# Half-row fetches, three-term products and twelve earlier slots in a hybrid decoder step

## The chip, the cores and the metric

The kernel runs on one core of a Trainium2 chip. The metric is device time in microseconds of one execution. Before the change the median of three runs is 1606.98 us (1599.02 to 1607.16). The core has a matrix engine (TensorE, PE in the profile, with its weight load shown apart as PEld), a vector engine (VectorE, DVE), a scalar engine (ScalarE, ACT), GpSimd (POOL), which also issues the indirect transfers, and SyncE (SP), which here issues most of the plain transfers. Sixteen DMA engines move the data.

## The reference

One layer of a decoder on 512 prompt tokens and 8 x 4 sample tokens. A projection feeds four retention heads and a convolution module; their outputs are mixed, added to the input and normalised, which gives `x1`. Then comes the part that the change touches, a retrieval of experts:

```python
q = (xb @ w_query).reshape(PEER_BLOCK, PEER_HEADS, PEER_DQ)
...
v1, i1 = lax.top_k(s1, PEER_TOPK)
v2, i2 = lax.top_k(s2, PEER_TOPK)
cand = (v1[..., :, None] + v2[..., None, :]).reshape(...)
sv, ci = lax.top_k(cand, PEER_TOPK)
idx = e1 * N_KEYS + e2
gate = jax.nn.softmax(sv)
u = jnp.take(peer_u, idx, axis=0)
act = jax.nn.gelu(jnp.einsum('phkd,pd->phk', u, xb), approximate=False)
vv = jnp.take(peer_v, idx, axis=0)
return jnp.einsum('phk,phkd->pd', gate * act, vv)
```

Each token picks 8 heads x 16 = 128 of 16384 experts. An expert is a row of 1024 numbers in each of two tables, `peer_u` and `peer_v`. The result is added to `x1` and normalised again.

## The kernel before, in words

The 544 tokens are treated in two ways. For 288 of them (128 first prompt tokens, the 32 sample tokens, 128 further prompt tokens) the chosen rows are **fetched**. For the last 256 (`ND`) prompt tokens all experts are computed **densely** and weighted with a matrix that is zero where an expert was not chosen.

*Fetched tokens.* `gather` (L567) handles a **slot** k: one chosen expert of each of 128 tokens. An indirect transfer on POOL's queue (L572) reads 128 rows of the joined table `uv` (8 KB each: 4 KB of `peer_u`, 4 KB of `peer_v`) into a tile `g`. DVE multiplies the first half with `x1` and sums it (the dot, L575), ACT makes the weight (L579, L580), and DVE adds the weighted second half to `acc` (L585). The tiles are three buffers in pool `gp`, and one more for some calls (`gx` for the first 60 slots, `gx2` in the last call), used for every fourth slot. There are 128 slots for the first prompt tokens (`I0`, in the profile `I`), 32 for the samples (`Is`: four experts of 32 tokens at a time) and 128 for the further prompt tokens (`Ib`).

*Dense tokens.* For each of 128 keys e, `scores_of` (L778) loads a 512 KB tile of the transposed first table and makes the 128 x 256 scores with 8 float32 products (L784). `v_stage` (L914) loads the matching 512 KB of `peer_v` into a tile `uv` (pool `uvp`, four buffers) and adds its 4 products of 128 x 512 to four accumulators `pB` (L920). The weight matrices are held in four buffers: `Gb` (keys 0 to 31), `Gc` (32 to 51), `Ga` (52 to 95), `Gd` (96 to 127). `build` (L855) makes the gate part of them out of one-hot factors: ACT makes `off` and `A` (L862, L864), DVE `M` and `B` (L866, L870), PE multiplies them (L875). `first_keys` (L888) does this for keys 0 to 95 and `last_keys` (L907) for 96 to 127. `s_stage` (L879) computes the scores of a key, applies Gelu and multiplies them into the buffer; it serves keys 32 to 51 inside `first_keys` and keys 96 to 127 late.

*Order.* The program's order is a suggestion: a planner simulates the program and writes down each engine's order of instructions, which is then fixed. Each engine takes its instructions strictly in that order. `phases` (L923) yields one `v_stage` at a time, with an `s_stage` of the last keys beside those after `last_keys` is through, and `run` (L965) alternates it with two slots of `fetched` (L944), which takes the 32 sample slots and then the 128 of the further prompt tokens. The **fence** (L576) is the last multiplication of `first_keys`: dots of the last call must stand behind it on DVE, and so must those of the sample call from slot `FREE` (12) on. At the end the two accumulator pairs are normalised and stored (L966).

Of the kernel before, what the change touches and what calls it, by code (L numbers as in the profile page):

```python
# [34 lines left out]
UV = 4  # L35
FREE = 12
EG = (32, 20, 44, 32)
# [56 lines left out]
def tile_step(ctx: ExitStack, tc: tile.TileContext, a, o):  # L94
# [472 lines left out]
    def gather(x1, idx, gate, acc, slots):  # L567

        for k in slots:
            spare = gx if x1 is x1_0 and k < KX else (gx2[0] if gx2 and len(slots) == 128 else None)  # L570
            t = (spare if spare is not None and k % 4 == 3 else gp).tile([128, 2 * D], F32, name="g")
            G.indirect_dma_start(out=t, out_offset=None, in_=a["uv"],  # L572
                                 in_offset=bass.IndirectOffsetOnAxis(ap=idx[:, k:k + 1], axis=0))
            act = gw.tile([128, 2], F32, name="act")
# [100 lines left out]
    for h0 in range(0, PH, 2):  # L675
        w = load_w(a["w_query"], h0 * 256)
        qq = small("qe", [128, 4, 128], bufs=1)
        for hs in ([h0], [h0 + 1]) if h0 == 0 else ([h0, h0 + 1],):
            for h in hs:
                for s in range(2):  # L680
                    m = (h - h0) * 2 + s
                    S.activation(qq[:, m], project(w, m, x1T0, 0, 128), AF.Copy)
            retrieve(lambda h, s: qq[:, (h - h0) * 2 + s], hs, 128, 1, E0, GT0, hs[0], led and (lambda ins: behind(ins, led[0])))
            ss = slice(hs[0] * TK, (hs[-1] + 1) * TK)
            c = V.tensor_copy(I0[:, ss], E0.rearrange("p h k -> p (h k)")[:, ss])
            led = led or [c]
# [103 lines left out]
    def topk_of(g, c0, which):  # L790
        w_, r_ = GSP[g]
        for h0 in which:
            retrieve(lambda h, s: qs[:, h * 2 + s, c0:c0 + w_], [h0] if r_ > 1 else [h0, h0 + 1], w_, r_, Eg[g], GTg[g], h0)
            ss = slice(h0 * TK, (h0 + (1 if r_ > 1 else 2)) * TK)
            V.tensor_copy(Ig[g][:, ss], Eg[g].rearrange("p h k -> p (h k)")[:, ss])

# [32 lines left out]
    for e in range(E0S[2], E0S[3]):  # L829
        S.activation(place(e), scores_of(e), AF.Gelu)  # L830
    gbs = ExitStack()
    gb = gbs.enter_context(tc.tile_pool(name="gb", bufs=1, side="right", reuse_waits="tile"))
    GW[0] = gb.tile([128, EG[0], ND], F32, name="Gb")
# [8 lines left out]
    dw_ = ctx.enter_context(tc.tile_pool(name="dw_", bufs=4, reuse_waits="tile"))  # L842
    gc = ctx.enter_context(tc.tile_pool(name="gc", bufs=1, reuse_waits="tile"))
    pacc = ctx.enter_context(tc.tile_pool(name="pacc", bufs=1, space=PSUM, reuse_waits="tile"))
# [62 lines left out]
    def last_keys():  # L907

        with tc.tile_pool(name="bt", bufs=2, reuse_waits="tile") as bt:
            for pt, ts in build(bt, E0S[3], EG[3], 16):  # L910
                S.activation(GW[3][:, :, ts], pt.rearrange("p t e -> p e t"), AF.Copy)
                yield

    def v_stage(e):  # L914
        vt = uvp.tile([128, D], F32, name="uv")
        nc.sync.dma_start(vt, a["uv"][e * NK:(e + 1) * NK, D:])
        W = place(e)
        for b in range(2):
            for q in range(2):
                T.matmul(pB[b][q], W[:, b * 128:(b + 1) * 128], vt[:, q * 512:(q + 1) * 512],  # L920
                         start=False, stop=(e == NK - 1), skip_group_check=True)

    def phases():  # L923
        for e in range(EG[0]):
            v_stage(e)
            yield
        gbs.close()
        gd = ctx.enter_context(tc.tile_pool(name="gd", bufs=1, side="right", reuse_waits="tile"))
        GW[3] = gd.tile([128, EG[3], ND], F32, name="Gd")
        b = last_keys()  # L930
        more = iter(range(E0S[3], NK))
        for e in range(E0S[1], E0S[3]):
            v_stage(e)
            if next(b, "end") == "end":
# [83 lines left out]
```

## Time and profile before

| | |
|---|---|
| median of three runs | 1606.98 us |
| the profiled execution | 1603.19 us, span 1601.4 us |
| mean granted TensorE clock | 0.971 |
| busy: PE, DVE, ACT, POOL | 93%, 77%, 38%, 23% of the span |
| moved by DMA | 503.75 MB, mean 315 GB/s |
| of that by indirect fetches (POOL's queue with some plain loads) | 305.12 MB |
| sample slots issued | 776.5 to 1065.3 us |
| last prompt slots (`Ib`) issued | 992.6 to 1567.4 us |
| v products (L920) | 949.6 us to 1585.9 us |
| score products (L784) | 492.1 us to 1406.9 us |

Times in the profile count from the start of the span. "Busy" for PE includes the drain of a product, so a busy PE need not be at its peak; where the pace of PE matters, the starts of successive instructions are compared. A float32 product appears as two instructions, each with a weight load. In a row that has "[0.60 <-ACT wgt L580]" the engine stood idle 0.60 us before the instruction, and what it waited for is named. A DMA share of 1.0 in a window means that all sixteen engines were busy with packets all the time.

### The profile page before, as it was taken

Reading aid. Unit: us, or ns where it says so; the run is one execution under the profiler, and the core shown is the slowest. Engines: PE = TensorE matmul, PEld = TensorE weight load, DVE = VectorE, ACT = ScalarE, POOL = GpSimd, SP = SyncE. Lnnn points to the kernel's source line nnn. Section 1 sums busy time; section 2 is a strip of 40 time slices with the busy share of each in tenths; the row PEclk is TensorE's granted clock in tenths of the full one; section 3 lists DMA queues with packets and bytes.
Section 4 is the critical chain, followed back from the end, with each engine's and each line's share of the span. In section 5 each row is a group of like instructions: output and inputs, shape, how many; then the busy total and the mean of one; then the engine's idle time right before and its main releaser. Section 6 shows DMA issues by size and latency. Waiting matters only on the chain.

```text
span 1601.4 us, 20802 instructions
## 1 busy us (share of the span) xinstructions
PE 1494.5 (93%) x7014; PEld 1010.1 (63%) x7014; DVE 1225.3 (77%) x3158; ACT 604.3 (38%) x1687; POOL 374.1 (23%) x335
## 2 busy tenths in 40 slices
PE   6899999996979999999999997999999999999996
PEld 6788556564756667788788875444566655543332
DVE  3939989989865999999852788566777777766666
ACT  2235542254222323333623888413994111111111
POOL 1001423444321222321120000122223222222221
PEclk9899999998989999999999997999999999999998
DMA  9458778997698669997794321998999999999995
GB/s 355 180 195 347 253 280 301 354 364 253 253 383 321 260 250 340 345 340 271 251 413 157 108 86 57 398 402 332 385 365 380 423 424 424 424 423 424 424 424 211
DMA packets 99543, 503.75 MB, mean 315 GB/s; under 512 B 10183, under 2 KB 21191, under 8 KB 56549
## 3 DMA queue, kind: packets, MB, share of 16 engines
q0 software_dynamic: 42240, 305.12, 48.7%
q1 hardware_dynamic: 50749, 189.96, 31.3%
q10 hardware_dynamic: 6448, 7.36, 1.5%
q8 instruction: 55, 0.90, 0.2%
q14 instruction: 51, 0.42, 0.1%
HBM read 497.03 MB, written 5.80 MB: 314 GB/s over the span
## 4 chain that ended last, share of the span: by engine, by line
PE 32%; DMA 28%; DVE 24%; issue 8%; ACT 4%; POOL 2%; SPq 0%; DVEq 0%; POOLq 0%; ACTq 0%
DMA g<-in_uv_dram,Ib 17%; PE pB L920 10%; PE sp L784 9%; PE mm L198 7%; DMA g<-in_uv_dram,I 7%; DVE acc L585 6%; DVE g L575 4%; POOL g L572 2%; ACT off L862 2%; PE mm L875 2%; PE mm L308 2%; DMA g<-in_w_in_dram 2%; DMA uv<-in_uv_dram 1%; DVE iu L504 1%; DVE score L505 1%
## 5 line engine op out<-in xcount | busy, mean ns | idle before, releaser
L784 PE MATMUL sp<-x1T,uv 128*128 128x256 f32 x2048 | 464.7, 384 | 15.4 <-ACT Ga L830 9.4
L784 PEld LDWEIGHTS sp<-x1T,uv 128*128 128x128 f32 x2048 | 385.5, 191 | 89.5 <-issue 23.2
L585 DVE SCALAR_TENSOR_TENSOR acc<-g,wgt,acc 128x1024 f32<-128x1024 f32 x285 | 365.0, 1281 | 99.3 <-ACT wgt L580 98.1
L572 POOL DMA_INDIRECT g<-in_uv_dram,I x128 | 181.9, 1421 | 435.1 <-DVE acc L585 222.6
L579 ACT ACTIVATE act<-act 128x1 f32<-128x1 f32 x288 | 57.9, 201 | 592.4 <-DVE g L575 592.0
L575 DVE SCALAR_TENSOR_TENSOR g<-g,x1g 128x1024 f32<-128x1024 f32 x160 | 195.3, 1224 | 94.2 <-DMA g<-in_uv_dram,Ib 63.1
L572 POOL DMA_INDIRECT g<-in_uv_dram,Ib x128 | 133.5, 1043 | 517.9 <-DVE acc L585 318.5
L575 DVE SCALAR_TENSOR_TENSOR g<-g,x 128x1024 f32<-128x1024 f32 x128 | 155.6, 1217 | 31.9 <-DMA g<-in_uv_dram,I 31.8
L198 PE MATMUL mm<-x1T,w 128*128 128x384 f32 (+1 forms) x512 | 176.1, 500 | 0.2 <-ACT score L524 0.2
L920 PE MATMUL pB<-uv,Ga 128*128 128x512 f32 x352 | 162.1, 604 | 1.1 <-DMA uv<-in_uv_dram 0.8
L862 ACT ACTIVATE off<-row,e1T 128x128 bf16<-128x128 bf16 x512 | 157.8, 388 | 1.5 <-PE mm L875 0.4
L198 PEld LDWEIGHTS mm<-x1T,w 128*128 128x128 f32 x512 | 96.6, 190 | 71.4 <-issue 37.9
L920 PE MATMUL pB<-uv,Gd 128*128 128x512 f32 x256 | 117.2, 601 | 2.1 <-DMA uv<-in_uv_dram 1.0
L920 PE MATMUL pB<-uv,Gb 128*128 128x512 f32 x256 | 115.4, 604 | 2.9 <-DMA uv<-in_uv_dram 2.5
L920 PEld LDWEIGHTS pB<-uv,Ga 128*128 128x128 f32 x352 | 63.7, 189 | 83.7 <-issue 63.1
L920 PEld LDWEIGHTS pB<-uv,Gd 128*128 128x128 f32 x256 | 46.1, 189 | 73.3 <-issue 48.2
L875 PEld LDWEIGHTS <-A 128*128 128x128 bf16 x1536 | 64.6, 100 | 36.6 <-issue 32.0
L920 PEld LDWEIGHTS pB<-uv,Gb 128*128 128x128 f32 x256 | 48.1, 193 | 59.6 <-issue 54.3
L875 PE MATMUL mm<-B,A 128*128 128x96 bf16 (+1 forms) x1536 | 68.4, 197 | 13.3 <-DVE Gc L901 12.4
L864 ACT ACTIVATE A<-off 128x1024 bf16<-128x1024 bf16 x64 | 67.4, 1053 | 28.1 <-PE mm L875 27.7
L870 DVE TENSOR_TENSOR B<-M,gtT 128x768 bf16<-128x768 bf16 (+1 forms) x192 | 69.8, 419 | 9.8 <-PE mm L875 9.6
L920 PE MATMUL pB<-uv,Gc 128*128 128x512 f32 x160 | 72.3, 599 | 0.0
(279 smaller groups left out, 1706.3 us busy)
## 6 DMA issues: line engine op xcount, KB each, us to landing
uv<-in_ut_dram SPq DMA_DIRECT2D x128, 512.0 KB
uv<-in_uv_dram SPq DMA_DIRECT2D x128, 512.0 KB
w<-in_w_in_dram SPq DMA_DIRECT2D x18, 1024.0 KB
w<-in_w_query_dram SPq DMA_DIRECT2D x16, 1024.0 KB
w<-in_w_out_dram SPq DMA_DIRECT2D x7, 1024.0 KB
g<-in_uv_dram,I POOLq DMA_INDIRECT x128, 7.9
keys<-in_state_retention_dram ACTq DMA_DIRECT2D x4, 512.0 KB
out_dram<-keys SPq DMA_DIRECT2D x4, 512.0 KB
```

The lines of the kernel that those rows point to most:

```text
L198: T.matmul(p[:, :n], w[m // 2][:, k, (m % 2) * 128:(m % 2 + 1) * 128], xT[:, k, c0:c0 + n], start=(k == 0), stop=(k == 7))
L308: mm = T.matmul(p[:n, q * 256:(q + 1) * 256], xT[:, k, c0:c0 + n], w[q][:, k, :], start=(k == 0), stop=(k == 7))
L572: G.indirect_dma_start(out=t, out_offset=None, in_=a["uv"], in_offset=bass.IndirectOffsetOnAxis(ap=idx[:, k:k + 1], axis=0))
L575: dot = V.scalar_tensor_tensor(t[:, :D], t[:, :D], 1.0, x1, op0=OP.mult, op1=OP.mult, accum_out=act[:, 0:1])
L579: S.activation(act[:, 1:2], act[:, 0:1], AF.Gelu)
L585: V.scalar_tensor_tensor(acc, v, wgt, acc, op0=OP.mult, op1=OP.add)
L784: T.matmul(sp, u[:, k], x1T[:, k, NG2:], start=(k == 0), stop=(k == 7))
L862: S.activation(off[:, t], row, AF.Abs, bias=e1T[:, t1 + t:t1 + t + 1])
L864: S.activation(A, off, AF.Relu, bias=1.0, scale=-1.0)
L870: V.tensor_tensor(B[:, q], M, pairs_of(gtT[:, q], t1).to_broadcast([128, TB // 2, ne, 2]), op=OP.mult)
L875: T.matmul(pt[:, t % nt], A[:, t - t1], B[:, q, (t - t1) // 2, :, t % 2], start=(q == 0), stop=(q == 2))
L920: T.matmul(pB[b][q], W[:, b * 128:(b + 1) * 128], vt[:, q * 512:(q + 1) * 512], start=False, stop=(e == NK - 1), skip_group_check=True)
```

## The change

1. A slot is fetched by two indirect transfers, one for each 4 KB half of the row: the table is viewed as twice as many rows of half the length, the indices are doubled when they are written (a `tensor_scalar` by 2.0 takes the place of a copy), and the second transfer has an element offset of one half row.
2. `v_stage` from key 52 on splits its operands. ACT copies the loaded tile to a float32r tile `vh` and the 128 x 256 weights to `Wh`; DVE subtracts to get the remainders `vl` and `Wl`, also float32r. Three products (`Wl` with `vh`, `Wh` with `vl`, `Wh` with `vh`) replace the one float32 product, so a key has 12 products of 128 x 512 in place of 4. Keys 0 to 51 are as before.
3. The split tiles live in a new pool `vhp` (two buffers of each), which takes the place of `Gc` once that has been used. To make this possible `Gd` is now the same buffer as `Gb`, and `gx2` moves to the other side of the memory.
4. `FREE` goes from 12 to 24: twelve more of the 32 sample slots may be worked on before the fence.

```diff
-FREE = 12
+FREE = 24
...
-            G.indirect_dma_start(out=t, out_offset=None, in_=a["uv"],
-                                 in_offset=bass.IndirectOffsetOnAxis(ap=idx[:, k:k + 1], axis=0))
+            for half in range(2):
+                G.indirect_dma_start(out=t[:, half * D:(half + 1) * D], out_offset=None, in_=a["uv"].rearrange("r (q d) -> (r q) d", q=2),
+                                     in_offset=bass.IndirectOffsetOnAxis(ap=idx[:, k:k + 1], axis=0), element_offset=half * D)
...
-            c = V.tensor_copy(I0[:, ss], E0.rearrange("p h k -> p (h k)")[:, ss])
+            c = V.tensor_scalar(I0[:, ss], E0.rearrange("p h k -> p (h k)")[:, ss], 2.0, None, op0=OP.mult)
...
-    gbs = ExitStack()
-    gb = gbs.enter_context(tc.tile_pool(name="gb", bufs=1, side="right", reuse_waits="tile"))
+    gb = ctx.enter_context(tc.tile_pool(name="gb", bufs=1, side="right", reuse_waits="tile"))
...
-    gc = ctx.enter_context(tc.tile_pool(name="gc", bufs=1, reuse_waits="tile"))
+    gcs = ExitStack()
+    gc = gcs.enter_context(tc.tile_pool(name="gc", bufs=1, reuse_waits="tile"))
...
         W = place(e)
+        if not vhp:
+            terms = ((W, vt),)
+        else:
+            vh, vl = vhp[0].tile([128, D], F32R, name="vh"), vhp[0].tile([128, D], F32R, name="vl")
+            S.activation(vh, vt, AF.Copy)
+            V.tensor_sub(vl, vt, vh.bitcast(F32))
+            Wh, Wl = vhp[0].tile([128, ND], F32R, name="Wh"), vhp[0].tile([128, ND], F32R, name="Wl")
+            S.activation(Wh, W, AF.Copy)
+            V.tensor_sub(Wl, W, Wh.bitcast(F32))
+
+            terms = ((Wl, vh), (Wh, vl), (Wh, vh))
         for b in range(2):
-            for q in range(2):
-                T.matmul(pB[b][q], W[:, b * 128:(b + 1) * 128], vt[:, q * 512:(q + 1) * 512],
-                         start=False, stop=(e == NK - 1), skip_group_check=True)
+            for w, v in terms:
+                for q in range(2):
+                    T.matmul(pB[b][q], w[:, b * 128:(b + 1) * 128], v[:, q * 512:(q + 1) * 512], start=False,
+                             stop=(e == NK - 1 and w is terms[-1][0] and v is terms[-1][1]), skip_group_check=True)
...
-        gbs.close()
-        gd = ctx.enter_context(tc.tile_pool(name="gd", bufs=1, side="right", reuse_waits="tile"))
-        GW[3] = gd.tile([128, EG[3], ND], F32, name="Gd")
+        GW[3] = GW[0]
...
+            if e == 52:
+                gcs.close()
+                vhp.append(ctx.enter_context(tc.tile_pool(name="vhp", bufs=2, reuse_waits="tile")))
...
-    gx2.append(ctx.enter_context(tc.tile_pool(name="gx2", bufs=1, reuse_waits="tile")))
+    gx2.append(ctx.enter_context(tc.tile_pool(name="gx2", bufs=1, side="right", reuse_waits="tile")))
```

More of the change, by code (lines that the diff above doesn't have):

```diff
@@ L794, in topk_of @@
             ss = slice(h0 * TK, (h0 + (1 if r_ > 1 else 2)) * TK)
-            V.tensor_copy(Ig[g][:, ss], Eg[g].rearrange("p h k -> p (h k)")[:, ss])
+            V.tensor_scalar(Ig[g][:, ss], Eg[g].rearrange("p h k -> p (h k)")[:, ss], 2.0, None, op0=OP.mult)
     for h0 in range(0, PH, 2):
@@ L912, in last_keys @@
                 yield
+    vhp = []
     def v_stage(e):
```

## The prediction

> **What bounds the kernel now.** I read the windows first (columns: length, busy time and count of PE, PEld, DVE, ACT, POOL, granted clock, DMA share, GB/s), to find which stages the change touches.
>
> ```profile
> 834.00:858.00 24.00, 24.00 (x113) 21.13 (x112) 0.38 (x1) 2.68 (x7) 0.94 (x1) 1.00 0.69 263
> 858.00:992.00 134.00, 118.30 (x1082) 101.57 (x1080) 101.59 (x381) 107.66 (x302) 0.00 (x0) 0.92 0.26 84
> 992.00:1092.00 100.00, 98.88 (x314) 44.41 (x315) 64.47 (x100) 33.66 (x98) 23.82 (x23) 0.98 0.95 373
> 1092.00:1199.00 107.00, 107.00 (x797) 60.00 (x797) 80.84 (x170) 89.94 (x262) 31.07 (x25) 1.00 0.94 365
> 1199.00:1407.00 208.00, 205.43 (x796) 127.50 (x794) 151.25 (x207) 50.88 (x175) 56.71 (x55) 1.00 1.01 415
> 1407.00:1582.00 175.00, 172.00 (x376) 67.36 (x375) 117.90 (x143) 23.78 (x95) 41.02 (x44) 1.00 0.99 413
> ```
>
> First keys run to the fence at about 992, sample slots to 1092, keys up to 51 to 1199; then a tail of 383 us holds keys 52 to 127 and the remaining slots, first with score products beside (to 1407), then without. Next the chain of waits (start, duration, what) for the tail, for the pace of PE, and the DMA view of 1400 to 1550:
>
> ```profile
> 895.98 1.04 PE mm L875 x24
> 897.01 3.52 PE sp L784 x16
> 1020.89 3.53 PE pB L920 x8
> 1024.78 3.53 PE pB L920 x8
> 1084.43 27.73 PE pB L920 x64
> 1522.89 11.42 DMA g<-in_uv_dram,Ib
> 1536.17 1.29 DVE acc L585
> 1537.72 11.42 DMA g<-in_uv_dram,Ib
> ```
> ```profile
> q0 software_dynamic: 5809, 42.31, 66.9%
> q1 hardware_dynamic: 5822, 21.22, 34.6%
> ```
>
> The tail's chain is transfer after transfer: 14.83 us from one to the next of the same buffer, four buffers, so 3.71 us for a slot, with all DMA engines busy. PE is close behind: 27.73/8 = 3.47 us for a key of v products, one key per slot. The two queues handle equal numbers of packets (5809 and 5822), 8 KB on POOL's queue and 4 KB on SP's. In engine time a slot (1.049 MB) costs 0.669 x 150 / 40.35 = 2.49 us, a tile (0.524 MB) 0.346 x 150 / 40.5 = 1.28 us; the shares sum to 1.015. How much the tail carries (dots with their accumulator reads, so two counts a slot; then the issues from 1199 to 1582):
>
> ```profile
> 1199.00:1407.00 208.00, 67.13 (x110) 1.00 1.01 415
> 1407.00:1582.00 175.00, 57.97 (x94) 1.00 0.99 413
> ```
> ```profile
> uv<-in_uv_dram SPq DMA_DIRECT2D x74, 512.0 KB
> uv<-in_ut_dram SPq DMA_DIRECT2D x27, 512.0 KB
> g<-in_uv_dram,Ib POOLq DMA_INDIRECT x99, 11.4
> ```
>
> So 102 slots are worked on and 99 issued, beside 101 tiles. (99 x 2.49 + 101 x 1.28)/1.015 = 370 of the 383 us: DMA bounds the tail, PE would bound it soon after, DVE has room. How DVE spends a slot there (idle before an instruction in brackets):
>
> ```profile
> 1538.06 1.22 DVE L575 SCALAR_TENSOR_TENSOR g<-g,x1g 128x1024 f32<-128x1024 f32 x1 [0.61 <-DMA g<-in_uv_dram,Ib]
> 1539.21 0.08 DVE L575 DVE_READ_ACCUMULATOR g<-g,x1g 128x1 f32 x1
> 1539.89 1.28 DVE L585 SCALAR_TENSOR_TENSOR acc<-g,wgt,acc 128x1024 f32<-128x1024 f32 x1 [0.60 <-ACT wgt L580]
> ```
>
> 1.15 us to the read, and 1.28: 2.43 us of work and 1.21 us of idle time, 0.60 for the weight and 0.61 for the next landing.
>
> **The change part by part.**
>
> *Twelve slots earlier.* They leave the tail and go ahead of the fence. Their gain in the tail is counted in its sum below: 87 issued, 90 worked on. Their new place:
>
> ```profile
> 833.09 1.28 DVE L585 SCALAR_TENSOR_TENSOR acc<-g,wgt,acc 128x1024 f32<-128x1024 f32 x1 [0.60 <-ACT wgt L580]
> 858.73 0.29 DVE L899 TENSOR_TENSOR Gb<-Gb,mm 128x128 f32<-128x128 f32 x1 [24.36 <-ACT Gb L835]
> POOL g L572 <- DVE Gc L899: 157.0, 1, 157.0
> ```
>
> The twelfth slot ends at 834 and DVE then idles 24.4 us until PE has made the scores of `Gb`; POOL's next issue waits 157 us for the fence. At 3.9 us a slot six of the twelve fit into that hole. The other six are 6 x 2.43 = 15 us of DVE in 858 to 992, where DVE is busy 102 of 134 us, and DMA is used to 0.26. The cover is PE's scores (118 of 134 us busy) and ACT (108). I charge +2 us; ends 0 (all covered) and +29 (none covered, 12 x 2.43). Behind the fence only 8 sample slots remain, so the last 128 begin some 50 us sooner; between 1092 and 1199 PE and ACT set the pace, and key 52 starts as before.
>
> *Two transfers a slot.* Bytes are the same. A 4 KB packet costs what a tile's does: 2 x 1.28 = 2.56 us of engines for a slot instead of 2.49. POOL issues twice:
>
> ```profile
> L572 POOL DMA_INDIRECT g<-in_uv_dram,I x128: 936/1071/7352, 129.7 to 738.1; - x128
> L572 POOL DMA_INDIRECT g<-in_uv_dram,Ib x128: 932/932/3545, 992.6 to 1567.4; - x128
> DVE g L575 <- DMA g<-in_uv_dram,I: 26.1, 22, 4.7
> ```
>
> One more issue is 0.93 us in the tail (POOL busy 41 of 175) and 1.07 us, at worst 7, in the front. There normalisations queue behind it on POOL, and later slots: perhaps six on the chain, 6 x 1.07 = +6 us at worst. Against it, a dot needs only the half issued first; DVE waited 26.1 us for landings between 130 and 500, and a quarter of that, 6 us, is the most I would credit. I take 0 for the front, ends -6 and +6. By packet counts, half-size packets give SP's tiles as many bytes as the slots where both queue, instead of half as many. In 1001 to 1036 PE started a key every 3.89 us (1020.89, 1024.78), waiting for tiles, instead of 3.53: nine such keys, -3 us. The doubled indices replace a copy by a multiply of the same size: nothing.
>
> The Trainium skill (DMA: Bandwidth & Descriptors, Queues, rings and completion order) says that each engine alternates between queues a packet at a time. The equal counts agree; what it would make of the tail is the second rival.
>
> *Three products.* No row shows a float32r product. A float32 one takes 3.47/4 = 0.87 us. The nearest row for a single pass is the bf16 one, 24 products of 96 columns in 1.04 us, or 0.231 us for 512 columns. I take 0.231 (the operands are rounded into float32r first, and the weight load of 0.19 us is shorter than that): 12 x 0.231 = 2.77 us for a key, instead of 3.47. The other end is 12 x 0.87 = 10.4 us.
>
> The Trainium skill (FP8 and Floating Point Precision, TensorE Precision Notes) says that true float32 makes four passes and that reduced float32 is truncated on reading; a quarter of 0.87 would give 2.60 us a key. No row here can show it.
>
> Each of the 76 keys adds work to ACT and DVE; nearest rows:
>
> ```profile
> L453 ACT ACTIVATE yt<-yt,lrs 128x1024 f32<-128x1024 f32 x2 | 2.5, 1240 | 9.6 <-DVE lrs L451 9.6
> L454 DVE TENSOR_TENSOR yt<-yt,lng 128x1024 f32<-128x1024 f32 x2 | 2.5, 1226 | 0.0
> L883 ACT ACTIVATE W<-sp 128x256 f32<-128x256 f32 x32 | 12.2, 380 | 52.0 <-PE sp L784 51.2 <-DVE Gd L886 0.8
> L886 DVE TENSOR_TENSOR Gd<-Gd,W 128x256 f32<-128x256 f32 x32 | 13.1, 422 | 1.8 <-ACT W L883 1.7
> ```
>
> ACT: 1.24 + 0.38 = 1.62 us a key, 123 us in a tail where it is busy 75 of 383; hidden, except that a slot's weight can queue behind a copy. DVE: successive instructions overlap by 0.08 us (1538.06 + 1.22 against 1539.21), so 1.14 + 0.34 = 1.48 us a key, 112 us. This stands on DVE's queue between dot and accumulation: a slot behind it comes later, and PE, which needed only the tile before, now waits for DVE.
>
> *The tail's new sum.* While scores are left (27 keys) PE needs 3.52 + 2.77 = 6.29 us a key, 170 us. DMA then moves 54 tiles (69 us) and, in what is left of 170 x 1.015, (172.6 - 69)/2.56 = 40 slots; DVE needs 40 x 2.43 + 27 x (1.48 + 0.34) = 146 us and fits. For the remaining 49 keys and 50 slots DVE needs 50 x 2.43 + 49 x 1.48 = 194 us, DMA (47 x 2.56 + 49 x 1.28)/1.015 = 180, PE 136: DVE bounds it. That is 364 us if subtractions fill the idle 1.21 us of every slot. ACT's queue costs some: 0.15 us a slot (a copy of 1.24 us in 4 us, half hit), 7 us. So 371 instead of 383: -12.
>
> *Memory.* The first split tile of key 52 waits for key 51's products on `Gc`, about 3 us once, hidden by score products already queued; `Gd` waited for `Gb` before too, as the pool was at the same place.
>
> **Sum.** -12 (tail) - 3 (tiles) + 2 (fence) + 0 (front) = -13 against the profiled 1603.2, whose span is 1601.4: 1590. The median of the runs stands 3.8 us above that execution, so 1594.
>
> **The rivals.**
>
> *First (slower): DVE's written order keeps its idle time.* If a subtraction stands ahead of a dot that has landed, or behind one that has not, idle time stays. Price: each idle 0.60 us kept in the 50 late slots adds 30 us to the 364, so 394, +11 with nothing else, near 1618; both kept, 425, near 1649. It decides from (383 - 364)/50 = 0.38 us per slot. For: DVE is strictly ordered and today idles 1.21 us in every slot. Against: the subtractions have two sets of tiles and can be placed in the holes.
>
> *Second (no difference): tiles first.* If both queues are always full, a tile comes every 2 x 1.28/1.015 = 2.52 us; 49 keys take PE's 2.77 us, 136 us, in which 29 slots are done, and 21 slots follow alone at 2.43 + 0.60: 64 us. With 170 and 7 that is 377, or 1600 to 1604. This is what the alternation named above leads to. Against: a key also needs DVE, whose order is written down.
>
> *Third (faster): DMA alone bounds the tail.* (87 x 2.56 + 101 x 1.28)/1.015 = 347, plus the 13 lost today: 360, -23; with -6 in front, 1575.
>
> *Fourth: the fence moves.* +15 to +29 instead of +2: 1607 to 1621. Against: the hole of 24 us.
>
> *Fifth: float32r is no faster.* From 0.33 us a product PE bounds the late part; at 0.87 it is over 500 us slower.
>
> **How the numbers follow.** My forecast 0.45 (own range 1583 to 1605), first 0.22, second 0.12, third 0.14, fourth 0.05, fifth 0.02. From no change a measurement tells about half a percent, 8 us, so faster means under 1599: 0.31 of my forecast, all of the third and a little of the second, 0.47. Same (1599 to 1615): 0.14, 0.10 and 0.04 of the first: 0.28. Slower: the rest, 0.25. The range: 1572, just under the third, to 1628, which holds the first with one hole kept and leaves out both kept.
>
> **What would show it.** A float32r product every 0.23 us; 24 sample dots ahead of 992 and the fence within some us of it; POOL's packets at 4 KB with as many bytes as SP's when both queue; in the tail DVE over 90% busy, PE with gaps that DVE ends, DMA below 1.0 after the scores. It is wrong if DVE keeps idle time per slot, if the last slots run alone, or if the fence is late by more than 10 us.

## The result and the profile after

The changed kernel takes 1649.72 us, median of four runs (1647.55 to 1656.95), against 1607.07 us of the kernel before measured beside it (four runs). The ratio is 1.0282, 95% interval [1.0242, 1.0322]: slower by 43 us where the prediction had 13 us faster, and above the range's end of 1628. The profiled execution took 1650.69 us (span 1648.9).

Landmarks come first. Rows of both kernels for one line each give count, minimum/median/maximum duration in ns, and the starts of the first and the last instruction: score products, the v products with `Gb` and `Gc`, and the copies into `Gd` of the kernel before,

```profile
L784 PE MATMUL sp<-x1T,uv x2048: 379/379/757, 492.1 to 1406.9; 128*128 128x256 f32 x187
L920 PE MATMUL pB<-uv,Gb x256: 592/592/1222, 949.6 to 1101.3; 128*128 128x512 f32 x128
L920 PE MATMUL pB<-uv,Gc x160: 592/592/676, 1101.7 to 1194.4; 128*128 128x512 f32 x160
L911 ACT ACTIVATE Gd<-mm x16: 573/577/597, 1101.9 to 1220.2; 128x512 f32<-128x512 f32 x16
```

and of the changed kernel (where `Gd` is the buffer `Gb`):

```profile
L785 PE MATMUL sp<-x1T,uv x2048: 376/379/634, 520.7 to 1462.3; 128*128 128x256 f32 x187
L937 PE MATMUL pB<-uv,Gb x256: 592/592/1219, 977.5 to 1126.1; 128*128 128x512 f32 x128
L937 PE MATMUL pB<-uv,Gc x160: 592/592/1200, 1126.5 to 1236.9; 128*128 128x512 f32 x160
L912 ACT ACTIVATE Gb<-mm x16: 570/576/597, 1141.6 to 1257.1; 128x512 f32<-128x512 f32 x16
L937 PE MATMUL pB<-vh,Wh x304: 387/389/632, 1254.6 to 1637.7; 128*128 128x512 f32 x152
```

The first score product comes 28.6 us later (520.7 against 492.1), before any key of the changed `v_stage` has run. `Gb`'s v products still are 28 us late at their start and 25 at their end; they take 148.6 us instead of 151.7. `Gc`'s last product is 42.5 us late, and the first copy into `Gd` 39.7. From the last `Gc` product to the last v product it is 400.8 us (1236.9 to 1637.7) instead of 391.5 (1194.4 to 1585.9). So the loss has three places: 28 us ahead of the scores (25 are left of them at the end of `Gb`), 17 more by the end of `Gc` (around 1126 to 1142), and 9 in the tail, where 12 were to be won. (That is 51.8 us at the last v product, of which the last normalisations give some back: 47.5 in the two spans.)

The same stages in the windows of the changed kernel (columns as in the prediction):

```profile
886.00:1018.00 132.00, 121.20 (x1107) 104.17 (x1105) 106.92 (x387) 109.58 (x309) 6.81 (x7) 0.95 0.38 131
1018.00:1118.00 100.00, 99.18 (x318) 44.83 (x318) 66.50 (x104) 35.47 (x103) 56.95 (x46) 0.99 0.94 359
1118.00:1242.00 124.00, 110.40 (x843) 61.81 (x842) 91.49 (x184) 96.54 (x285) 72.39 (x58) 0.94 0.98 368
1242.00:1462.00 220.00, 195.19 (x858) 150.78 (x857) 188.40 (x260) 81.58 (x218) 163.29 (x110) 0.97 1.00 392
1462.00:1592.00 130.00, 105.64 (x397) 76.01 (x397) 121.87 (x157) 59.66 (x128) 82.58 (x56) 0.95 0.97 373
1592.00:1638.00 46.00, 43.90 (x183) 33.05 (x181) 29.20 (x40) 20.27 (x29) 0.80 (x2) 1.00 0.46 147
```

In the tail DVE is at 94% (121.87 of 130) once the scores are through, as forecast. While scores run, DMA is full (1.00) and PE idles 25 of 220 us. Then comes what was not forecast: from 1592 no slot is left, the DMA share is 0.46, and the last keys run by themselves. It holds the subtractions of 15 keys, and the copies of ten of those keys (first and last of the ten) start 25.81 us apart, 2.87 us a key:

```profile
1606.50 1.06 ACT L927 ACTIVATE vh<-uv 128x1024 fp32r<-128x1024 f32 x1 [2.10 <-PE pB L937]
...
1632.31 1.06 ACT L927 ACTIVATE vh<-uv 128x1024 fp32r<-128x1024 f32 x1 [1.39 <-PE pB L937]
```

The new instructions, by form (count, then busy time and mean ns, then idle time before them):

```profile
L928 DVE TENSOR_TENSOR vl<-uv,vh 128x1024 fp32r<-128x1024 f32 x76 | 92.7, 1221 | 17.3 <-ACT vh L927 17.3
L927 ACT ACTIVATE vh<-uv 128x1024 fp32r<-128x1024 f32 x76 | 79.3, 1045 | 21.2 <-PE pB L937 20.1 <-issue 1.1
L937 PE MATMUL pB<-vl,Wh 128*128 128x512 f32 x304 | 104.1, 424 | 20.7 <-DVE vl L928 20.3
```

And the queues between 1300 and 1450 (packets, MB, share of sixteen engines):

```profile
q0 software_dynamic: 11033, 40.19, 67.1%
q1 hardware_dynamic: 5730, 20.88, 34.7%
```

Packets are 4 KB on both queues, but the slots' queue now sends 11033 of them and the tiles' 5730. Bytes stand at 2:1 as before. Engine time is 0.671 x 150 / 38.3 = 2.63 us for a slot (40.19 MB are 38.3 slots) and 0.347 x 150 / 39.8 = 1.31 us for a tile.

In front, GpSimd. For each kernel: the waits of its queue from 130 to 500 (total us, times, longest); then, from 130 to the first score product, the busy time of all engines, and DVE's dots alone (two counts a slot). Before:

```profile
POOL g L572 <- DVE acc L585: 179.1, 61, 8.4
```
```profile
130.00:492.10 362.10, 326.42 (x1391) 224.93 (x1390) 314.52 (x691) 136.85 (x348) 130.76 (x97) 0.95 0.86 317
130.00:492.10 362.10, 96.66 (x158) 0.95 0.86 317
```

And after:

```profile
POOL g L573 <- DVE acc L586: 53.3, 30, 4.7
POOL g L573 <- issue: 32.1, 105, 0.7
```
```profile
130.00:520.70 390.70, 331.45 (x1399) 228.14 (x1399) 331.37 (x720) 141.97 (x363) 241.28 (x190) 0.92 0.87 310
130.00:520.70 390.70, 104.03 (x170) 0.92 0.87 310
```

Before, GpSimd waited 179.1 us for accumulations, that is for a buffer to come free. After, it waits 53.3 us for them and is busy 241.28 instead of 130.76 us, with 0.3 us more between two issues (32.1 us in 105 gaps). The slots do not come slower by that: DVE has done the dots of 80 slots by 500 us in both kernels. It is the other work that comes late. Ahead of the first score product stand 85 slots' dots instead of 79; six slots at 2.43 us are 15 of the 17 us that DVE is busy longer, and it is idle 59 instead of 48 us.

### The profile page after: what moved, and what is told of

It is laid out like the page before. It is cut to its first block, busy times and chain, and to the rows that moved or that the text cites. A ratio compares the mean times of both kernels' runs of the same rounds, so it can differ in the third digit from the quotient of the medians.

```text
span 1648.9 us, 22151 instructions
## 1 busy us (share of the span) xinstructions
PE 1466.4 (89%) x7318; PEld 1079.2 (65%) x7318; DVE 1331.5 (81%) x3310; ACT 704.2 (43%) x1839; POOL 800.6 (49%) x623
## 4 chain that ended last, share of the span: by engine, by line
DVE 21%; PE 20%; DMA 11%; POOL 10%; issue 10%; ACT 7%; DVEq 0%; POOLq 0%; ACTq 0%
POOL g L573 10%; PE sp L785 10%; PE pB L937 5%; DMA g<-in_uv_dram,Ib 5%; DVE acc L586 5%; DVE g L576 4%; DMA g<-in_uv_dram,I 4%; ACT off L863 3%; PE mm L198 3%; DMA g<-in_uv_dram,Is 2%; PE mm L876 2%; DVE vl L928 1%; ACT A L865 1%; DVE iu L504 1%; DVE B L871 1%
## 5 line engine op out<-in xcount | busy, mean ns | idle before, releaser
L573 POOL DMA_INDIRECT g<-in_uv_dram,Ib x256 | 363.1, 1418 | 276.2 <-PE mm L876 110.9
L573 POOL DMA_INDIRECT g<-in_uv_dram,I x256 | 333.3, 1302 | 270.3 <-DVE acc L586 100.6
L576 DVE SCALAR_TENSOR_TENSOR g<-g,x1g 128x1024 f32<-128x1024 f32 x160 | 194.8, 1221 | 32.0 <-DMA g<-in_uv_dram,Is 17.0
L573 POOL DMA_INDIRECT g<-in_uv_dram,Is x64 | 77.1, 1205 | 98.5 <-DVE sv L506 35.9
L937 PE MATMUL pB<-vl,Wh 128*128 128x512 f32 x304 | 104.1, 424 | 20.7 <-DVE vl L928 20.3
L937 PE MATMUL pB<-vh,Wl 128*128 128x512 f32 x304 | 91.8, 417 | 30.6 <-ACT vh L927 27.9
L928 DVE TENSOR_TENSOR vl<-uv,vh 128x1024 fp32r<-128x1024 f32 x76 | 92.7, 1221 | 17.3 <-ACT vh L927 17.3
L937 PE MATMUL pB<-vh,Wh 128*128 128x512 f32 x304 | 98.6, 407 | 0.0
L937 PEld LDWEIGHTS pB<-vh,Wl 128*128 128x128 f32 x304 | 54.8, 193 | 58.3 <-ACT vh L927 43.5
L927 ACT ACTIVATE vh<-uv 128x1024 fp32r<-128x1024 f32 x76 | 79.3, 1045 | 21.2 <-PE pB L937 20.1
L937 PEld LDWEIGHTS pB<-vl,Wh 128*128 128x128 f32 x304 | 55.8, 195 | 49.6 <-DVE vl L928 39.9
```

Source lines behind the costliest of these rows:

```text
L573: G.indirect_dma_start(out=t[:, half * D:(half + 1) * D], out_offset=None, in_=a["uv"].rearrange("r (q d) -> (r q) d", q=2), in_offset=bas ...
L576: dot = V.scalar_tensor_tensor(t[:, :D], t[:, :D], 1.0, x1, op0=OP.mult, op1=OP.mult, accum_out=act[:, 0:1])
L927: S.activation(vh, vt, AF.Copy)
L928: V.tensor_sub(vl, vt, vh.bitcast(F32))
L937: T.matmul(pB[b][q], w[:, b * 128:(b + 1) * 128], v[:, q * 512:(q + 1) * 512], start=False, stop=(e == NK - 1 and w is terms[-1][0] and v ...
```

## The experiments

Diffs are against the kernel named in each. Each ratio is that of the kernel's runs to runs of the kernel before on the same chip, with its 95% interval.

**Which part costs: one part undone, one part alone.**

`whole_rows`: the changed kernel with one 8 KB transfer a slot.

```diff
-            for half in range(2):
-                G.indirect_dma_start(out=t[:, half * D:(half + 1) * D], ...)
+            G.indirect_dma_start(out=t, out_offset=None, in_=a["uv"], ...)
```

> The changed kernel with one 8 KB transfer a slot again; three products and 24 slots kept. Theory O (written order): the planner lets more slots go ahead of other work, and what stands behind them on a queue is late. Here 76 slots, as before the change (81 with halves), stand ahead of the last normalisation on POOL, so the first score product is back near 492 us (520 in the changed kernel); but 18 of the last call's weights still stand ahead of the first copy into Gd on ACT (4 before, 20 changed), so that copy stays 10 to 16 us behind PE's last Gb product, and 5 keys instead of 15 are left after the last slot: 1598 to 1612 us. Theory Q (the second issue on POOL is the whole loss, order matters little): all of it is given back, 1585 to 1597 us.

1607.62 us, ratio 1.0014 [0.9996, 1.0032]. The total lies in theory O's range, but the late copy that O needs is not there: the first copy into `Gb` starts at 1102.6, 3 us after `Gb`'s last product (1099.4). `halves_only` is the opposite, the kernel before with the two transfers (and doubled indices):

```diff
-            G.indirect_dma_start(out=t, out_offset=None, in_=a["uv"], ...)
+            for half in range(2):
+                G.indirect_dma_start(out=t[:, half * D:(half + 1) * D], ...)
```

> The kernel before with two transfers a slot and nothing else. Theory O: 81 slots ahead of the last normalisation, first score product near 520 us (492 before), 4 weights ahead of the first Gd copy, so nothing is lost there, and the last slots are bound by DMA as before: 1628 to 1642 us. Theory Q: the front loses the same 28 us, and every later slot is slower too, because POOL needs 2 x 1.9 us for it: 1645 to 1665 us.

1643.7 us, ratio 1.0251 [1.0216, 1.0286], between the two ranges. `no_split` is the changed kernel with the float32 product for all keys:

```diff
-            if e == 52:
-                gcs.close()
-                vhp.append(...)
```

> The changed kernel with the single float32 product for all keys; halves and 24 slots kept. Theory O: front late by 28 us, first Gd copy late by 15 us (20 weights ahead of it), then a tail with 12 fewer slots and PE at 3.47 us a key without DVE's subtractions: 1615 to 1630 us. If the three products were the loss instead: 1590 to 1605 us.

1646.04 us, ratio 1.0263 [1.0234, 1.0292], above both ranges. `free24_only` is the kernel before with 24 slots ahead of the fence:

```diff
-FREE = 12
+FREE = 24
```

> The kernel before with 24 slots ahead of the fence and nothing else. Theory O: the fence stays within 3 us of 992, but 18 weights stand ahead of the first Gd copy on ACT (4 before), which comes 10 to 16 us late, and the tail is 25 to 30 us shorter: 1588 to 1602 us. If the written order there costs nothing: 1574 to 1584 us.

1597.77 us, ratio 0.9954 [0.9938, 0.997], in theory O's range, though its first copy into `Gd` is not 10 to 16 but 3 us later than before (1104.6). So the two transfers carry the whole loss: without them nothing is left (1.0014), and alone they cost 2.5%. The twelve earlier slots by themselves gain 0.5%, the only part that does; the three products cost that much again (1.0014 against 0.9954; with two transfers a slot, 1.0282 against 1.0263, the intervals overlap).

To see where the transfers cost, `first_whole` is the changed kernel with whole rows in the first call (`I`) and halves in the two later ones:

```diff
-            for half in range(2):
-                G.indirect_dma_start(out=t[:, half * D:(half + 1) * D], ...)
+            if x1 is x1_0:
+                G.indirect_dma_start(out=t, out_offset=None, in_=a["uv"], ...)
+            else:
+                for half in range(2):
+                    G.indirect_dma_start(out=t[:, half * D:(half + 1) * D], ...)
```

> The changed kernel with one 8 KB transfer a slot in the first call and two of 4 KB in the other two. Theory A, the front carries nearly all of what two transfers cost: the first score product comes at 494-500 and the fence at 990-995 as with whole rows everywhere, and the rest is only the dearer packets (up to 10 us): ratio 1.002 to 1.008. Rival B, the later calls lose as much as the front (the copies into Gd, the longer issue beside the subtractions): first score product as in A, but ratio 1.012 to 1.020.

1613.69 us, ratio 1.0061 [1.0035, 1.0087]; the first score product comes at 495.4. Theory A holds: 1.0282 - 1.0061 = 0.022, 35 us give or take 8 by the intervals, is the first call's, and 1.0061 - 1.0014 = 0.005, 8 us give or take 5, that of the two later calls.

**Why the front is late.** The planner writes more slots ahead of each of the eight late normalisations in GpSimd's order (36, 51, 54, 61, 69, 71, 77, 81 instead of 34, 51, 54, 59, 66, 68, 72, 76). `pinned_front` is `halves_only` with the old counts enforced (50 for the second one).

```diff
+                if x1 is x1_0 and k >= AHEAD[0]:
+                    behind(fetch, norms[1 + sum(n <= k for n in AHEAD)])
```

> Two transfers a slot on the kernel before, as in halves_only, but the eight late normalisations of the front are pinned on POOL behind 34, 50, 54, 59, 66, 68, 72 and 76 slots, as in the kernel before (36, 51, 54, 61, 69, 71, 77 and 81 in halves_only). Theory O (the planner's order): the first score product is back at or before 500 us (492 before, 519 in halves_only), and the total at 1615 to 1628 us, the rest being the dearer 4 KB packets. Theory P (two issues occupy POOL for about 3 us a slot, so normalisations wait whatever their place): first score product at 508 to 519 us, total 1630 to 1645 us.

```profile
L785 PE MATMUL sp<-x1T,uv x2048: 379/379/757, 518.9 to 1435.5; 128*128 128x256 f32 x187
```
```profile
L789 PE MATMUL sp<-x1T,uv x2048: 379/379/483, 514.2 to 1425.3; 128*128 128x256 f32 x187
```

1628.8 us, ratio 1.0146 [1.012, 1.0172]. The first score product moves from 518.9 to 514.2, 5 of the 27 us there. That is within the scatter: in `no_split`, with the same counts as `halves_only`, it stands at 511.7. But the total falls by 1.0251 - 1.0146 = 0.0105, 17 us give or take 7; the profiled executions show 8 at `Gb`'s first product and 10 at the last v product. So the order bears on the loss, and how much the runs do not fix. The first score product is in theory P's range and the total between the two ranges. `tiny_second` is the kernel before with an added transfer of 256 bytes a row into an unused tile after each slot of the first call, and no halves:

```diff
+            if x1 is x1_0:
+                bit = gw.tile([128, 64], F32, name="bit", bufs=4)
+                G.indirect_dma_start(out=bit, out_offset=None, in_=a["uv"], ...)
```

> The kernel before with whole 8 KB rows, and in the first call a second indirect transfer a slot that brings 256 bytes a row into a scratch tile that nothing reads: POOL issues as often as with halves, and the packets of the rows stay whole. 72 slots stand ahead of the last normalisation (76 before). Theory P: first score product at 505 to 525 us, total 1620 to 1645 us. Theory O: with fewer slots ahead it comes at 480 to 496 us, and the total stays within 8 us of 1606 us.

Its score products and DVE's wait for slots (130 to 500):

```profile
L788 PE MATMUL sp<-x1T,uv x2048: 379/379/634, 533.8 to 1441.0; 128*128 128x256 f32 x187
```
```profile
DVE g L579 <- DMA g<-in_uv_dram,I: 43.2, 20, 6.9
```

1638.39 us, ratio 1.0224 [1.0195, 1.0252]. With a sixteenth of a half row and only 72 slots ahead of the last normalisation, the scores start later than in any other run, 533.8. So a second transfer is enough for such a loss, without bytes to speak of and with whole rows; whether GpSimd's time for the issue or its 128 further packets do it, this run does not separate. It does not repeat the front of the changed kernel either. The small transfers run ahead (the last is issued at 454.6), so all 128 of them stand ahead of the last normalisation, and here the slots are slower: 69 dots by 500 us instead of 80, with 43.2 us of waits for landings instead of 26.1. From 130 to 520 GpSimd is busy 276 of 390 us; up to 500 there are 36.8 us of gaps ahead of the small issues.

A second issue can hurt in two ways: normalisations queue behind it on GpSimd, or the slots themselves come slower. `halves_off_pool` and `whole_off_pool` take the normalisations off GpSimd, with two transfers and with one: the addition runs on DVE and the power of -0.5 is left out.

```diff
-        G.tensor_scalar(dst, var, EPS, None, op0=OP.add)
-        G.tensor_tensor(dst, dst, mhalf[:dst.shape[0]].to_broadcast(list(dst.shape)), op=OP.pow)
+        V.tensor_scalar(dst, var, EPS, None, op0=OP.add)
```

> The kernel before with two 4 KB transfers a slot, and the normalisations taken off GpSimd: the addition of epsilon runs on VectorE and the power of -0.5 is left out (so the normalised values are scaled otherwise and other experts are chosen; the work is the same). To be compared with the same edit on one 8 KB transfer. Theory P1, the front is late because normalisations queue behind the issues on GpSimd: the first score product comes within 8 us of the one with whole rows. Theory P2, the doubled issues slow the slots themselves, and with them the vector work ahead of the mix stage: 15 to 28 us stay between the two.

> The kernel before (one 8 KB transfer a slot) with the normalisations taken off GpSimd in the same way; the measure for the run with two transfers. By P1 the normalisations also waited behind single issues of about 1 us, so the first score product comes up to 8 us ahead of 492; by P2 within 3 us of 492, unless the planner writes another order.

```profile
L784 PE MATMUL sp<-x1T,uv x2048: 379/379/796, 522.9 to 1426.5; 128*128 128x256 f32 x187
```
```profile
L783 PE MATMUL sp<-x1T,uv x2048: 379/379/757, 502.5 to 1408.0; 128*128 128x256 f32 x187
```

20.4 us stay between the two, inside P2's band: most of the delay does not need the normalisations in GpSimd's queue. P2's reason does not hold either, as the slots are not slower: 81 dots by 500 us with two transfers, 80 with one. Ahead of the first score product stand 85 dots instead of 80, and five slots at 2.43 us are 12 us of DVE's time. So more slots are written and done ahead of the other work, with or without normalisations on GpSimd; what the rest of the 20 us is stays open. Neither of them started earlier than with the normalisations on GpSimd (the pair has other expert choices and an order of its own, so only the difference is used). 1632 and 1604 us, one execution each.

**The late copy into `Gd`.** In the changed kernel ScalarE's written order has 20 slot weights ahead of the first copy. `gd_ahead` puts the weights from the seventh slot on behind it.

```diff
+            if fence and len(slots) == 128 and k >= 6:
+                later.append(out)
...
+                for ins in later:
+                    behind(ins, gd)
```

> The changed kernel, with the weights of the last call's slots from the seventh on ordered behind the first copy into Gd on ScalarE (in the changed kernel 20 of them stand ahead of that copy, here 6). Theory Q, the written order of ScalarE costs the stage: in the changed kernel the copy runs at 1141.6, 15 us after PE has started its last Gb product (1126.1); here it follows that product within 5 us, Gc's last product starts near 1222 instead of 1237, and the total falls by about 15 us to 1630-1640. Rival R, the copy's place only shows that DMA and the slots are the limit there: Gc's products come sooner, but the slots held back are late by as much, and the total stays within 5 us of 1650.

The copies, and the window of PE's first idle time in the changed kernel, there and here:

```profile
L914 ACT ACTIVATE Gb<-mm x16: 570/575/597, 1125.8 to 1248.4; 128x512 f32<-128x512 f32 x16
```
```profile
1126.00:1145.00 19.00, 19.00 (x91) 9.01 (x90) 11.75 (x15) 5.58 (x18) 11.37 (x11) 1.00 0.86 307
```
```profile
1126.00:1145.00 19.00, 6.89 (x25) 3.09 (x24) 12.70 (x16) 3.95 (x14) 11.82 (x10) 0.70 1.01 402
```

The copy runs at 1125.8 and PE idles no more (busy 19.00 of 19 us, instead of 6.89). `Gc`'s last product starts at 1225.7 instead of 1236.9. But the total is 1646.65 us, ratio 1.0279 [1.0241, 1.0317], as in the changed kernel. Rival R holds: the late copy cost nothing that a measurement shows. DMA was full in that window (1.01); that the slots worked on meanwhile are missing later is the likely reason, and not shown.

**Why the three products gain nothing.** In `whole_rows`, without the halves, the tail from `Gc` to the last v product is 1201.0 to 1592.7, 392 us as before. Its two stretches, and the queues (packets, MB, share) in the first:

```profile
1201.00:1428.50 227.50, 197.02 (x874) 159.09 (x872) 188.21 (x257) 78.77 (x210) 83.29 (x56) 0.94 0.98 385
1428.50:1575.00 146.50, 126.02 (x512) 96.17 (x511) 142.43 (x188) 73.88 (x155) 51.89 (x31) 0.98 0.98 383
```
```profile
q0 software_dynamic: 7903, 57.54, 64.1%
q1 hardware_dynamic: 8198, 29.86, 33.8%
```

57.54 MB are 55 slots and 29.86 MB are 57 tiles: one slot for one tile, as before the change. 28 keys took 227 us, 8.1 us each. PE's waits from 1204 to 1595, and the largest wait of SyncE's queue in the first stretch:

```profile
PE pB L936 <- ACT vh L926: 32.0, 15, 3.8
PE pB L936 <- DVE vl L927: 18.1, 28, 1.4
```
```profile
SPq L781 <- DVE vl L927: 75.8, 14, 9.0
```

With 2.8 us for the weights' remainders PE waits 53 us, where the kernel before waited 1.8; the three products save 76 x 0.63 = 48. A tile's buffer now comes free when DVE has subtracted, no longer when PE is through with it, and the request for the next tile waits for that. The granted clock of 0.94 in the first stretch takes, by estimate, another 0.06 x 227.5 = 14 us of PE's full speed.

`five_tiles` gives `whole_rows` a fifth tile buffer.

```diff
-UV = 4
+UV = 5
-    dw_ = ctx.enter_context(tc.tile_pool(name="dw_", bufs=4, reuse_waits="tile"))
+    dw_ = ctx.enter_context(tc.tile_pool(name="dw_", bufs=3, reuse_waits="tile"))
```

> whole_rows with five tile buffers instead of four (and three instead of four buffers for the Gelu results of a key, to make room). Theory T (with scores left the tiles come too slowly, as four buffers share a queue that gets a third of the bytes): a key with scores takes 6.5 to 6.9 us instead of 7.5, the last score product comes at 1405 to 1418 us instead of 1428, total 1590 to 1602 us. Theory D (DVE bounds the tail throughout): last score product within 5 us of 1428, total 1603 to 1612 us.

```profile
1390.00:1536.00 146.00, 136.53 (x577) 107.77 (x576) 143.71 (x187) 76.74 (x155) 53.62 (x31) 0.99 0.98 380
1536.00:1600.00 64.00, 0.21 (x1) 0.00 (x0) 51.44 (x67) 9.94 (x40) 26.86 (x17) 0.54 0.79 290
```

```profile
q0 software_dynamic: 5807, 42.33, 58.2%
q1 hardware_dynamic: 7834, 28.50, 38.9%
```

1615.44 us, ratio 1.0066 [1.004, 1.0092], above both ranges. The queues are those from 1201 to 1389.5: 40 slots and 54 tiles, so the ratio follows the buffers (or the order that the planner writes for them). The last score comes at 1389.7 instead of 1428.4, so the supply of tiles did pace the keys. Now the keys end at 1536, DVE having been busy 143.71 of 146 us, and the slots left over run 60 us by themselves.

`split_late`, `split_112` and `split_odd` are `whole_rows` with the products in three terms only for keys 104 to 127, for keys 112 to 127, and for the odd keys.

```diff
-        if not vhp:
+        if e < 104:
```
```diff
-        if not vhp:
+        if e < 112:
```
```diff
-        if not vhp:
+        if e < 52 or e % 2 == 0:
```

> Whole rows and 24 slots, and the three products only for keys 104 to 127. In free24_only the slots end at 1532 us and PE goes on alone to 1588 us. If the split pays only where DVE and the tiles have room: 24 keys at 2.87 instead of 3.47 us are 14 us less, 1582 to 1592 us. If the split never pays: 1594 to 1606 us.

1599.74 us, ratio 0.9979 [0.9959, 0.9998]: no gain over 24 slots alone (0.9954), as the second range had it.

> The changed kernel with one 8 KB transfer a slot, 24 slots ahead of the fence, and the three products only for keys 112 to 127. With 24 slots alone the slots ended at 1532 and PE then ran 56 us by itself, 16 keys of 3.5 us. Theory T, the split pays once no slots run beside it: 16 keys of 2.87 us (the pace of the changed kernel's last keys) take 46 us, so the total falls 10 us below that of 24 slots alone, to a ratio near 0.989 (0.986 to 0.992). Rival U, a split key costs as much as a plain one wherever it stands, because its tile must land and be split before PE starts: 0.995 to 0.999, as when keys 104 to 127 were split (0.9979).

1597.74 us, ratio 0.9965 [0.9943, 0.9987]. In `free24_only` the slots are through at 1532 and PE then runs alone. A window after that, first of it and then of `split_112` (the number after POOL is the granted clock):

```profile
1534.00:1545.00 11.00, 11.00 (x27) 4.88 (x26) 4.96 (x8) 1.24 (x1) 0.80 (x2) 1.00 0.56 174
```
```profile
1534.00:1545.00 11.00, 8.74 (x25) 6.66 (x26) 7.47 (x12) 4.12 (x5) 0.80 (x2) 0.69 0.48 152
```

The split keys do run at 2.84 us each (four copies start at 1550.86 to 1559.39). But at the first of them PE waits 2.6 us for the copy and the subtraction (waits of PE from 1530 to 1590), and the granted clock of that window is 0.69:

```profile
PE pB L936 <- DVE vl L927: 1.6, 1, 1.6
PE pB L936 <- ACT vh L926: 1.0, 1, 1.0
```

The last v product stands at 1585.1 instead of 1588.2: of 16 x 0.63 = 10 us, 3 are left in the profiled executions. The wait and the slower clock, by estimate (1 - 0.69) x 11 = 3.4 us, account for most of the rest. The ratios don't tell the two kernels apart. Theory T had the pace right and not the total, which is rival U's.

> The changed kernel with one 8 KB transfer a slot and the three products only for the odd keys from 53 to 127; the even ones have the plain product. PE saves 38 x 0.63 = 24 us, and VectorE has half of the subtractions: 87 x 2.43 + 38 x 1.48 + 27 x 0.34 = 277 us in a tail of some 385, 72% instead of 88%. Theory D, VectorE's load made the split worthless (with all 76 keys it was 97 to 99% busy): with half of it the tail ends up to 20 us sooner than with 24 slots alone, ratio 0.982 to 0.990. Rival V, the order of tiles and slots sets the end (one slot for one tile, the last keys by themselves) and the split gives back in waits what it saves: 0.993 to 1.000, as with the last 24 keys (0.9979) and the last 16 (0.9965).

1607.61 us, ratio 1.0021 [0.9996, 1.0045], on the slower side even of rival V. ScalarE's copy of the tile, and what it waited for from 1204 to 1595, and the engines after the scores:

```profile
L926 ACT ACTIVATE vh<-uv 128x1024 fp32r<-128x1024 f32 x38 | 39.8, 1049 | 47.6 <-DMA uv<-in_uv_dram 47.6
```
```profile
1417.00:1546.00 129.00, 110.52 (x325) 63.79 (x324) 104.56 (x134) 38.11 (x100) 44.05 (x30) 0.95 0.99 396
```

In `whole_rows` DVE was the limit after the scores, as forecast (142.43 of 146.5 us). Here it is busy 104.56 of 129 us, 81%, and the kernel is no faster, so DVE's load alone is not the reason. The copies wait 47.6 us for tiles to land, and PE, which could start a plain product as the tile lands, waits for the copy: from 1200 to 1590 17.8 us for copies, 4.6 for subtractions and 11.1 for the plain keys' tiles, 33.5 us in all, where the split saves 24.

## Why the prediction was wrong

The forecast -13 was a sum of four terms. Two of them failed, and a third no run shows.

*The front, taken as 0 between -6 and +6: +28 at the first score product, +35 (give or take 8) in the total.* This step failed. It priced the second issue as "perhaps six on the chain, 6 x 1.07 = +6 us at worst". The slots took the second issues without delay: the 93 instructions more that GpSimd has up to the first score product take 110 us and the gaps 32, and its wait for free buffers gives way from 179 to 53 us. The row that said so was quoted (128 issues, 936/1071/7352 ns); what was left out was to add them, and to ask what stands beside the slots. That is the work that came late. Until the first score product DVE has six more slots to do, 15 us, and idles 12 us longer. The runs bound the causes: the old order of the normalisations gives back 5 us at the first score product and 17, give or take 7, in the total (`pinned_front`); 20 us stay with none of them on GpSimd. How much of the 28 us is the planner's order and how much GpSimd's time is not taken apart by a run. The credit for a first half that lands early did not show: DVE's wait for landings from 130 to 500 is 30.6 us instead of 26.1.

*The tail, taken as -12: 0 with whole rows, +9 as changed.* The duration of a product was right: 0.231 us forecast, 2.87/12 = 0.24 at the end, where keys run by themselves. A quarter of the float32 product, by the four passes that the Trainium skill (FP8 and Floating Point Precision, TensorE Precision Notes) states, was an estimate of 2.60 us a key and comes out 9% too short. The copies and subtractions were right too (1045 and 1221 ns for the large ones), and they filled DVE's holes after the scores (94%, and 97% with whole rows). So the first rival did not happen there; that its 1649, with both holes kept, meets the measured 1649.72 is luck, as most of the loss lies in the front.

What failed is the step "DMA then moves 54 tiles and, in what is left, 40 slots" in 170 us. With whole rows it was 57 tiles and 55 slots in 227 us, from `Gc`'s end to the last score. The other division by itself costs the sum nothing: at the forecast's prices (57 x 1.28 + 55 x 2.49)/1.015 = 207, and 34 slots and 48 keys are left, 34 x 2.43 + 48 x 1.48 = 154 for DVE, 361 in all instead of 364. The term that was mis-sized is the price of a transfer. 1.28 and 2.49 were read where nothing was split; beside the split the engines, 0.98 busy, moved 385 GB/s instead of 415, by which the 207 us become 223 of the 227. `five_tiles` had the forecast's own load, 54 tiles and 40 slots, and took 188 us. Why transfers take longer beside the split no run takes apart. And PE did not set the pace, but waited 53 us for copies and subtractions, about what the three products save. When the slots are through early, the last keys run alone (15 in the changed kernel, with DMA at 0.46); moved the other way (`five_tiles`), the slots run alone. "The last slots run alone" was named as a sign against the forecast; in the changed kernel it was the last keys.

*The tiles, -3:* `Gb`'s 32 keys take 148.6 instead of 151.7 us, but 150.7 in `halves_only` and 152.3 in `no_split`, which have the same packets. So no run shows this term. The second rival stood on equal packets of two queues that are always full (the alternation that the Trainium skill states in DMA: Bandwidth & Descriptors, Queues, rings and completion order); the counts are 11033 to 5730. The packet times of the traces show that "always full" failed. Before the change, from 1250 to 1400, at least two packets of each queue are in flight all the time, and 5815 and 5813 start. After it, from 1300 to 1450, that is so in 0.66 of the time, in which 5857 and 5358 start; for the rest one queue, nearly always the tiles', has next to nothing in flight. This agrees with an alternation while both have work, but does not prove it: in `whole_rows` 4983 and 6582 start in such times (1201 to 1428.5), and the records don't tell one engine's packets from another's.

*The fence, +2:* the 24 slots stand ahead of it, and `free24_only` reaches `Gb`'s products at 949.1 instead of 949.6 us and issues the first slot of the last call at 990.4 instead of 992.6. Nothing at the fence, then, and inside the ends; but `Gc`'s last product comes 7.5 us later (1201.9 instead of 1194.4), which no term held. The sign "the fence is late by more than 10 us" did come (1018), by way of the front.

*Packets of half the size:* as forecast, 2.57 us a slot in `halves_only` from 1300 to 1450 (0.672 x 150 / 39.2) for 2.56, and 1.28 a tile. The rest of the 2.63 of the changed kernel goes with the split: beside it whole rows take 2.64 (and tiles 1.34) in the same stretch. The two later calls cost 8 us. The longer wait for `Gd`, forecast as nothing, was 16 us at the copy and nothing in the total (`gd_ahead`).

The faster kernel of this study is `free24_only`, 0.9954. It frees the slots 49 us sooner (last accumulation 1532.3 instead of 1581.6), but PE then bounds the tail, so little of that reaches the end.

## What to carry to other kernels

Price an added issue by its sum over the stage and not by those that happen to be quoted on the chain. Hold that sum against the issuing engine's waits, which may take it up for the fetched data themselves, and look at what other work stands behind the issues in the engines' order: here that work was late and the slots were not. Take the price of a transfer from a stretch in which the new work runs beside it. Here, with the DMA engines full, slots and tiles came about one to one with four buffers of each, and 40 to 54 with five tile buffers. The faster products gained nothing, as PE waited for copies and subtractions for as long as it saved, and these held each tile's buffer until DVE was through.

## What the runs showed of the hardware that was not expected

GpSimd's indirect issues have no fixed length. From 1300 to 1450 (count, busy us and mean ns, idle time), first `free24_only` and `whole_rows`, both with one 8 KB transfer a slot, then `pinned_front`, with two of 4 KB and no subtractions:

```profile
L572 POOL DMA_INDIRECT g<-in_uv_dram,Ib x41 | 41.9, 1021 | 111.3 <-DVE acc L585 95.8 <-DMA g<-in_uv_dram,Ib 15.5
```
```profile
L572 POOL DMA_INDIRECT g<-in_uv_dram,Ib x38 | 57.9, 1522 | 94.0 <-DVE acc L585 92.6 <-DMA g<-in_uv_dram,Ib 1.3
```
```profile
L575 POOL DMA_INDIRECT g<-in_uv_dram,Ib x79 | 108.0, 1368 | 40.6 <-DVE acc L590 21.7 <-issue 18.3 <-DMA g<-in_uv_dram,Ib 0.6
```

1021 ns without the subtractions and 1522 with them; but 1368 in `pinned_front`, where DVE is busy 105 of 150 us, as in the kernel before (106), whose issues take 933. So neither the subtractions nor a higher load on VectorE is needed for a long issue. The Trainium skill (SBUF — State Buffer, Who interferes with whom) says that a two-input `tensor_tensor` shares only a read interface with GpSimd and, as an inference, doesn't stall the writing of descriptors; these runs neither bear that out nor contradict it. What sets the length was not tried.

Transfers moved less in the same time beside the split, with the engines as busy: from 1300 to 1450 424 GB/s in the kernel before (DMA share 1.02) and 394 in `whole_rows` (0.99).

In `split_112` the granted clock fell after two waits of PE of 1.0 and 1.6 us, in a stretch at 1.00. Windows of 2 us read 0.62, 0.50 and 0.50 from 1536 to 1542, the last two with PE busy all the time, and the window from 1545 to 1548 reads 1.00 again; that is the 0.69 of the 11 us. The plain keys of `free24_only` kept 1.00 there.
